# Merging two of three split passes in the mixers' feature-major gemms

## The chip, the cores and the metric

The kernel runs on one core of one Trainium2 chip. The metric is the device time of one execution in microseconds, and times are given as medians of several runs. Before the change the median of 3 runs is 1141.07 us (1139.65 to 1142.34).

## What is computed

Two transformer blocks run one after the other on 256 tokens with 1024 features, all in f32. The first mixes tokens by two kinds of attention with learned biases and has an MLP; the second has two gated FFNs around a mixer of dilated attention and an mLSTM. What the change touches are the two mixers' input projections:

```python
proj = h @ w_in[l]                       # block 1: queries, keys, values, gates
q_a, k_a, v_a, q_i, k_i, w_i, q_b, kv_b, g_b, g_br = jnp.split(proj, split_pts, axis=-1)
...
mix = (jax.nn.sigmoid(gate_a) * (o_a @ w_branch_a[l])
       + jax.nn.sigmoid(gate_b) * (o_b @ w_branch_b[l]))
x = x + mix @ w_out[l]
...
qk = jax.nn.silu(causal_depthwise_conv(qk_m, conv_w, conv_b))      # block 2
merged = jax.nn.sigmoid(g_a) * (att @ w_att_branch) + jax.nn.sigmoid(g_m) * (ml @ w_mlstm_branch)
```

Block 2's projection has the same form; it yields q, k, v of the dilated attention, the conv's input, the mLSTM's v and output gate, and two branch gates.

## The kernel before

**The split.** Every f32 product is made of three products of rounded parts: with w = hi + lo and x = xh + xl it adds hi·xh, hi·xl and lo·xh. Weights come from HBM in units of 1024 columns per partition (512 KB), issued by SyncE five units ahead (`stream_dma`). `stream_split` makes the parts two units ahead: ScalarE copies raw to `hi` (L262), VectorE subtracts to `lo` (L263). The activations lie in SBUF as `both`, of which `hi` and `lo` parts are halves that stand side by side for each k-tile.

**Three kinds of gemm.** `gemm_tok` (L305 to L307) puts tokens on the output partitions. `gemm_feat` puts features there: for each k-tile and feature tile it issues three passes of 256 columns, L349 (hi·xh), L351 (hi·xl), L352 (lo·xh), into one half of a PSUM bank; a chunk is 512 weight columns, four feature tiles, two banks. `gemm_pair`, used in the MLP and the FFNs, issues one pass of 512 columns (L368: hi against xh and xl together) and one of 256 (L369), and adds the two halves afterwards (ScalarE copy L373, VectorE add L374).

**After a gemm.** A `done` function takes the finished bank. In the mixers it multiplies by `rsB`, the norm's reciprocal root per token, on VectorE straight from PSUM: L1252 (block 2's q and k), L958 (block 1's gates), L1441 (conv input `xc`), L1470 (block 2's gates). Then follow, in block 2's q and k, the rope on GpSimd (two DMAs into `sw`, then L1260 to L1262); in the conv ScalarE's and VectorE's taps (L1446, L1449), a tanh, and GpSimd's L1453 and L1454.

**Order.** Side work (attention steps, biases, compressed keys, mLSTM heads) waits in `self.pending` and is put between k-steps by `flush`. TensorE's, VectorE's and ScalarE's instructions are then ordered by a scheduler that simulates a timeline; GpSimd and SyncE keep the program's order. Three PSUM banks (`pacc`) hold gemm results.

**Places that matter.** Block 1: the bias table goes L589 (TensorE), L591 (`tv`, VectorE), two DMAs issued by GpSimd (`tvd`, `BT`), `cmpB` (L600), `gek`, then L766; attention steps score (L835), normalize, and multiply by values (L868), the last into `oa` (L802), which is transposed (L399) and split (L406, L407) into `oaT` for the branch gemm. Block 2: L1353 multiplies the roped q and k; the mLSTM heads are multiplied into `hm` (L1521), transposed by L399.

Of the kernel before, what the change touches and what calls it, by code (L numbers as in the profile page):

```python
# [9 lines left out]
F32 = mybir.dt.float32  # L10
# [11 lines left out]
D = 1024  # L22
KT = 2
# [73 lines left out]
W_IN1 = Wt("w_in", D, [352] + [512] * 3 + [352] + [512] * 4)  # L97
# [13 lines left out]
W_G2 = Wt("ffn2_w_gate_2", D, FFW, 4)  # L111
W_U2 = Wt("ffn2_w_up_2", D, FFW, 4)
# [97 lines left out]
class Prog:  # L210
# [8 lines left out]
    def plan(self):  # L219

        o = [(W_IN1, c) for c in (4, 0, 1, 3, 2, 5, 6, 7, 8)]
# [11 lines left out]
        o += [(W_IN2, c) for c in (6, 0, 1, 2, 3, 4, 5, 7, 8, 9, 14, 15, 16, 17, 10, 18, 12, 19, 11, 13, 20, 21)]  # L233
# [124 lines left out]
    def gemm_pair(self, W, c, x, done, rate=1, delay=0):  # L358
# [16 lines left out]
        done(s)  # L375

# [176 lines left out]
    def block1_mix(self, x0, x):  # L553
        tc, nc, ap, g = self.tc, self.nc, self.ap, self.g
        with ExitStack() as es, ExitStack() as rs_:
# [78 lines left out]
            self.gemm_tok(W_IN1, 4, *xT, small_done, acc=self.psm)  # L634
# [5 lines left out]
            def d0(i, ps):  # L640
                if i == 0:
                    nc.vector.tensor_tensor(qi, ps, bc2, op=ALU.mult)
                else:
                    nc.vector.tensor_tensor(ki[64:96, :], ps[64:96, 0, :], rsB[64:96, :], op=ALU.mult)
                    nc.vector.tensor_tensor(ka[0:64, :], ps[0:64, 0, :], rsB[0:64, :], op=ALU.mult)
                    for p in (0, 32, 96):
                        nc.gpsimd.dma_start(ki[p:p + 32, :], ki[64:96, :])
                    nc.gpsimd.dma_start(ka[64:128, :], ka[0:64, :])
            self.later(rsB_job)
            self.gemm_feat(W_IN1, 0, *xT, d0)  # L650
# [130 lines left out]
            self.gemm_feat(W_IN1, 2, *xT, dq(qa))  # L781
# [173 lines left out]
            def gdone(c):  # L955
                def f(i, ps):
                    gsl = gate[:, 4 * c + 2 * i:4 * c + 2 * i + 2, :]
                    nc.vector.tensor_tensor(gsl, ps, bc2, op=ALU.mult)  # L958
                    nc.scalar.activation(gsl, gsl, AF.Tanh, scale=0.5)
                    nc.gpsimd.tensor_scalar(gsl, gsl, 0.5, 0.5, op0=ALU.mult, op1=ALU.add)  # L960
                return f
            for c in range(4):
                self.gemm_feat(W_IN1, 5 + c, *xT, gdone(c))
# [232 lines left out]
    def mixer2(self, x):  # L1196
        tc, nc, ap, g = self.tc, self.nc, self.ap, self.g
        xT, js = self.nextT
        with ExitStack() as es, ExitStack() as rs_:
# [237 lines left out]
            def cdone(c):  # L1437
                def f(i, ps):
# [143 lines left out]
```

## Time and profile before

| | |
|---|---|
| median of 3 runs | 1141.07 us |
| the profiled execution's own time | 1140.78 us |
| its span in the profile | 1139.0 us |
| mean granted TensorE clock | 0.990 |
| TensorE (PE) busy | 1112.4 us, 6848 passes |
| VectorE (DVE) busy | 766.9 us |
| ScalarE (ACT) busy | 573.3 us |
| GpSimd (POOL) busy | 143.8 us |

The span is measured on the chip between the first and last instruction; the execution's own time is 1.8 us longer. Passes of TensorE overlap, so the duration of one pass in the profile is longer than the distance from its start to the next one's. The pace is read from starts. A releaser behind "<-" is what ended an engine's wait.

### The profile page before, as it was taken

The numbers are of one execution on the slowest core, as the hardware profiler recorded it, in microseconds if no ns is written. First come the engines' busy times: TensorE is split into PE (matmuls) and PEld (weight loads), VectorE is DVE, ScalarE is ACT, GpSimd is POOL, SyncE is SP. The second block draws the span as 40 slices with busy tenths as digits, with TensorE's granted clock in tenths as the row PEclk, the third lists the DMA queues.
The fourth block names the chain that finished last, engine by engine and source line by source line (L and its number), as shares of the span: only waits on it lengthen the run. The fifth ranks groups of instructions, "written<-read, shape, count | busy, mean of one in ns | idle before, by whom it ended". The sixth has DMA issues, their size and how long they took to land.

```text
span 1139.0 us, 17655 instructions
## 1 busy us (share of the span) xinstructions
PE 1112.4 (98%) x6848; PEld 993.6 (87%) x6848; DVE 766.9 (67%) x1208; ACT 573.3 (50%) x858; POOL 143.8 (13%) x145
## 2 busy tenths in 40 slices
PE   8989999999999999999999999999999999999997
PEld 8888899888888888888878998889999987888886
DVE  6755776778764568777457676556779777776644
ACT  6324454555544446555446335555555455655542
POOL 1411230000000010000001784000323000000000
PEclk9998999999999999999999999999999998999999
DMA  8792214655555655555555655434545455555552
GB/s 294 255 195 97 65 51 146 200 187 187 191 196 173 201 181 187 186 184 192 195 167 184 192 179 167 162 119 145 185 149 166 166 188 167 185 186 186 188 179 92
DMA packets 55876, 196.91 MB, mean 173 GB/s; under 512 B 6700, under 2 KB 6972, under 8 KB 55536
## 3 DMA queue, kind: packets, MB, share of 16 engines
q1 hardware_dynamic: 52704, 186.44, 49.9%
q0 software_dynamic: 2800, 9.21, 3.3%
q8 instruction: 54, 0.88, 0.3%
q14 instruction: 30, 0.25, 0.1%
q10 hardware_dynamic: 288, 0.14, 0.1%
HBM read 192.84 MB, written 1.44 MB: 171 GB/s over the span
## 4 chain that ended last, share of the span: by engine, by line
PE 85%; POOL 5%; DMA 4%; DVE 4%; ACT 1%; issue 1%; DVEq 0%; SPq 0%; POOLq 0%; ACTq 0%
PE acc L368 20%; PE acc L369 10%; PE acc L307 9%; PE acc L306 9%; PE acc L305 9%; PE acc L349 6%; PE acc L351 6%; PE acc L352 6%; PE sm L835 2%; POOL sw L1261 2%; DMA sw<-qkT 2%; POOL qkT L1262 2%; POOL qkT L1260 1%; PE o L868 1%; DVE lo L263 1%; DMA BT<-tvd 1%
## 5 line engine op out<-in xcount | busy, mean ns | idle before, releaser
L263 DVE TENSOR_TENSOR lo<-raw,hi 128x1024 fp32r<-128x1024 f32 (+2 forms) x356 | 450.0, 1267 | 272.1 <-ACT hi L262 270.2
L262 ACT ACTIVATE hi<-raw 128x1024 fp32r<-128x1024 f32 (+2 forms) x356 | 371.5, 1045 | 432.9 <-issue 133.4
L368 PE MATMUL acc<-xs,hi 128*128 128x512 f32 x960 | 340.3, 400 | 1.3 <-DVE sum L374 1.1
L369 PE MATMUL acc<-xs,lo 128*128 128x256 f32 x960 | 269.0, 281 | 1.6 <-DVE lo L263 1.6
L368 PEld LDWEIGHTS acc<-xs,hi 128*128 128x128 f32 x960 | 180.8, 189 | 44.6 <-DVE sum L374 1.3
L349 PE MATMUL acc<-xs,hi 128*128 128x256 f32 (+1 forms) x696 | 199.8, 289 | 0.3 <-ACT hi L262 0.3
L351 PE MATMUL acc<-xs,hi 128*128 128x256 f32 (+1 forms) x696 | 199.0, 287 | 0.0
L352 PE MATMUL acc<-xs,lo 128*128 128x256 f32 (+1 forms) x696 | 198.1, 287 | 0.1
L369 PEld LDWEIGHTS acc<-xs,lo 128*128 128x128 f32 x960 | 181.9, 189 | 2.3 <-DVE lo L263 1.9
L349 PEld LDWEIGHTS acc<-xs,hi 128*128 128x128 f32 (+1 forms) x696 | 133.6, 192 | 3.7 <-issue 2.5
L351 PEld LDWEIGHTS acc<-xs,hi 128*128 128x128 f32 (+1 forms) x696 | 133.7, 192 | 2.4 <-issue 2.0
L352 PEld LDWEIGHTS acc<-xs,lo 128*128 128x128 f32 (+1 forms) x696 | 132.9, 192 | 1.6 <-issue 1.0
L306 PE MATMUL acc<-lo,hT 128*128 128x512 f32 x304 | 118.5, 390 | 0.0
L307 PE MATMUL acc<-hi,hT 128*128 128x512 f32 x304 | 118.0, 389 | 0.0
L305 PE MATMUL acc<-hi,hT 128*128 128x512 f32 x304 | 117.8, 390 | 0.0
L307 PEld LDWEIGHTS acc<-hi,hT 128*128 128x128 f32 x304 | 57.1, 188 | 11.9
L305 PEld LDWEIGHTS acc<-hi,hT 128*128 128x128 f32 x304 | 57.1, 188 | 11.8
L306 PEld LDWEIGHTS acc<-lo,hT 128*128 128x128 f32 x304 | 57.1, 188 | 11.7
L305 PE MATMUL acc<-hi,xs 128*128 128x386 f32 (+1 forms) x128 | 48.6, 381 | 1.6 <-DVE f L1129 1.5
L306 PE MATMUL acc<-lo,xs 128*128 128x386 f32 (+1 forms) x128 | 47.9, 374 | 0.0
L307 PE MATMUL acc<-hi,xs 128*128 128x386 f32 (+1 forms) x128 | 47.0, 373 | 0.0
L374 DVE TENSOR_TENSOR sum<-acc,sum 128x512 f32<-128x512 f32 x60 | 41.1, 684 | 0.0
(421 smaller groups left out, 1396.6 us busy)
## 6 DMA issues: line engine op xcount, KB each, us to landing
raw<-in_w_in SPq DMA_DIRECT2D x100, 512.0 KB, 3.5
raw<-in_ffn_w_gate SPq DMA_DIRECT2D x44, 512.0 KB, 3.4
raw<-in_ffn_w_up SPq DMA_DIRECT2D x44, 512.0 KB, 3.3
raw<-in_ffn_w_down SPq DMA_DIRECT2D x44, 512.0 KB, 3.4
raw<-in_w_mlp_in SPq DMA_DIRECT2D x32, 512.0 KB, 3.4
raw<-in_w_mlp_out SPq DMA_DIRECT2D x32, 512.0 KB, 3.3
raw<-in_w_out SPq DMA_DIRECT2D x16, 512.0 KB, 3.5
raw<-in_w_in SPq DMA_DIRECT2D x16, 386.0 KB, 3.3
```

Source lines behind the costliest of these rows:

```text
L262: nc.scalar.activation(hi[:, :n * w], raw[:, :n * w], AF.Copy)
L263: nc.vector.tensor_tensor(lo[:, :n * w], raw[:, :n * w], hi[:, :n * w], op=ALU.subtract)
L305: nc.tensor.matmul(ps[t][:, :w], xh[:, k, sl], hi, start=(k == 0), stop=False)
L306: nc.tensor.matmul(ps[t][:, :w], xh[:, k, sl], lo, start=False, stop=False)
L307: nc.tensor.matmul(ps[t][:, :w], xl[:, k, sl], hi, start=False, stop=last)
L349: nc.tensor.matmul(o, hi[:, fs], xh[:, k, :], start=(k == 0 and f % 2 == 0), stop=False, skip_group_check=True)
L351: nc.tensor.matmul(o, hi[:, fs], xl[:, k, :], start=False, stop=False, skip_group_check=True)
L352: nc.tensor.matmul(o, lo[:, fs], xh[:, k, :], start=False, stop=last, skip_group_check=True)
L368: nc.tensor.matmul(ps[:, f, :, :], hi[:, fs], x.both[:, k, :, :], start=(k == 0), stop=False)
L369: nc.tensor.matmul(ps[:, f, 0, :], lo[:, fs], x.hi[:, k, :], start=False, stop=last)
L374: nc.vector.tensor_tensor(s, ps[:, :, 0, :], s, op=ALU.add)
L835: nc.tensor.matmul(ps[:, i, :], q[pr:pr + 64, U["fts"][i], t * 128:t * 128 + 128], kk, start=True, stop=True)
```

## The change

A new function `gemm_half` does the mixers' feature-major gemms. Chunks are 256 columns wide, two feature tiles, and each tile has a PSUM bank of its own. A unit still holds 1024 columns, now four k-tiles of 256. For each k-tile there is one pass of 512 columns (hi against xh and xl) and one of 256 (lo·xh); at the tile's end ScalarE copies the half that holds hi·xl to SBUF, and VectorE adds the other half to it. When both tiles are there, `done` multiplies by `rsB` from SBUF: on VectorE as before for queries, keys and block 2's gates, on GpSimd for block 1's gates and the conv's input. 87 feature tiles change, 31 of block 1 and 56 of block 2. The branch gemms stay with `gemm_feat`, and the token-major chunks keep their widths. `flush` is called once per tile and unit, 8 times in 512 columns where `gemm_feat` called it 7 times.

```diff
-        self.kt, kts = k // 128, kt
+        self.kt = k // 128
...
+            kts = 1 << (UNIT // w).bit_length() - 1
...
-W_IN1 = Wt("w_in", D, [352] + [512] * 3 + [352] + [512] * 4)
+W_IN1 = Wt("w_in", D, [256, 96] + [256] * 6 + [352] + [256] * 8)
...
-W_IN2 = Wt("w_in_2", D, [512] * 6 + [VIF] * 4 + [512] * 12)
+W_IN2 = Wt("w_in_2", D, [256] * 12 + [VIF] * 4 + [256] * 8 + [512] * 4 + [256] * 8)
...
+    def gemm_half(self, W, c, x, dst, done, rate=1, delay=0):
+        nc = self.nc
+        w = W.widths[c]
+        nf = -(-w // 128)
+        ps = [self.pacc.tile([128, 512], F32, tag="acc", name="acc") for _ in range(nf)]
+        for u in range(len(W.off[c])):
+            kts = self.load_unit(W, c, u)
+            for f in range(nf):
+                n = min(128, w - 128 * f)
+                o = ps[f][:n, :].rearrange("p (a t) -> p a t", a=2)
+                for k, hi, lo in kts:
+                    fs = slice(f * 128, f * 128 + n)
+                    nc.tensor.matmul(o, hi[:, fs], x.both[:, k, :, :], start=(k == 0), stop=False)
+                    nc.tensor.matmul(o[:, 0, :], lo[:, fs], x.hi[:, k, :], start=False, stop=(k == W.kt - 1))
+                if kts[-1][0] == W.kt - 1:
+                    d = dst(f)
+                    nc.scalar.activation(d, o[:, 1, :], AF.Copy)
+                    nc.vector.tensor_tensor(d, o[:, 0, :], d, op=ALU.add)
+                    if f == nf - 1:
+                        done()
+                if delay <= kts[0][0]:
+                    self.flush(rate)
...
-            self.gemm_feat(W_IN1, 1, *xT, d1)
+            for c in range(2):
+                self.gemm_half(W_IN1, 2 + c, xT, lambda f: kv[:, 2 * c + f, :], lambda: kvdone(c))
...
-                    nc.vector.tensor_tensor(gsl, ps, bc2, op=ALU.mult)
+                nc.gpsimd.tensor_tensor(gsl, gsl, bc2, op=ALU.mult)
...
-            for c in range(6):
-                self.gemm_feat(W_IN2, c, *xT, qkdone(c % 2, c // 2))
+            for c in range(12):
+                i, gr, j = c // 2 % 2, c // 4, c % 2
+                self.gemm_half(W_IN2, c, xT, lambda f: qkT[i][:, gr, 2 * j + f, :], lambda: qkdone(i, gr, j))
...
-                    nc.vector.tensor_tensor(xc[:, :, 4:260], ps, rsB.unsqueeze(1).to_broadcast([128, 2, 256]),
-                                            op=ALU.mult)
+                        nc.gpsimd.tensor_tensor(th, th, bc2, op=ALU.mult)
```

The order of the instructions shifts with it. TensorE at the end of block 1, before the change: `oa` are the attention's outputs of the two token halves, `obT` the transposed parts of the other branch; the last `o<-tms,PT` stands 62 rows further up.

```order
L351 MATMUL acc<-obT_1061,hi 128x256
L352 MATMUL acc<-obT_1060,lo 128x256
L399 MATMUL sm<-ident,oa_1065 128x128
L399 MATMUL sm<-ident,oa_1066 128x128
L349 MATMUL acc<-obT_1060,hi 128x256
L351 MATMUL acc<-obT_1061,hi 128x256
L352 MATMUL acc<-obT_1060,lo 128x256
L349 MATMUL acc<-obT_1060,hi 128x256
L351 MATMUL acc<-obT_1061,hi 128x256
L352 MATMUL acc<-obT_1060,lo 128x256
L399 MATMUL tr<-ident,oa_1065 128x128
L399 MATMUL tr<-ident,oa_1066 128x128
```

And in the changed kernel, where L426 is the transpose and L900 the pass with the values:

```order
L354 MATMUL acc<-obT_972,lo 128x256
L351 MATMUL acc<-obT_972,hi 128x256
L900 MATMUL o<-tms,PT 128x64 x8
L353 MATMUL acc<-obT_973,hi 128x256
L354 MATMUL acc<-obT_972,lo 128x256
L351 MATMUL acc<-obT_972,hi 128x256
L353 MATMUL acc<-obT_973,hi 128x256
L354 MATMUL acc<-obT_972,lo 128x256
L426 MATMUL sm<-ident,oa_977 128x128
L426 MATMUL sm<-ident,oa_978 128x128
L426 MATMUL tr<-ident,oa_977 128x128
L426 MATMUL tr<-ident,oa_978 128x128
```

The last pass with the values now stands 5 branch passes ahead of the transposes, which come in a row; before, more than 60 branch and gate passes lay between, and the transposes were spread among branch passes.

TensorE in block 2, before: the first product of roped q and k (`qkT`, L1353) stands among the value gemm's passes, behind the whole gemm of q and k.

```order
L305 MATMUL acc<-hi,xs 128x386
L306 MATMUL acc<-lo,xs 128x386
L307 MATMUL acc<-hi,xs 128x386
L1353 MATMUL sm<-qkT_5816,qkT_5815 128x256
L305 MATMUL acc<-hi,xs 128x386
L306 MATMUL acc<-lo,xs 128x386
```

In the changed kernel (L1383 is that product, L393 and L394 the gemm of q and k) it stands inside the gemm of q and k, after 120 of its 192 pairs; the second stands after 184.

```order
L394 MATMUL acc<-xs,lo 128x256
L393 MATMUL acc<-xs,hi 128x512
L394 MATMUL acc<-xs,lo 128x256
L1383 MATMUL sm<-qkT_5640,qkT_5639 128x256
L393 MATMUL acc<-xs,hi 128x512
L394 MATMUL acc<-xs,lo 128x256
```

So TensorE now comes to the first two of these products earlier, and to the third with 103 instead of 96 passes of the value gemm behind it.

GpSimd in the conv, two tiles' worth of instructions, before (`xc` is the conv's padded input, `y` its sum, `qkm` its result):

```order
L1440 MEMSET xc 128x2x4
L1453 TENSOR_SCALAR xc<-xc 128x2x256
L1454 TENSOR_TENSOR qkm_7595<-xc,y 128x512
L1440 MEMSET xc 128x2x4
L1453 TENSOR_SCALAR xc<-xc 128x2x256
L1454 TENSOR_TENSOR qkm_7595<-xc,y 128x512
```

And in the changed kernel, where the multiply by `rsB` (L1475) stands ahead of each pair:

```order
L1471 MEMSET xc 128x2x4
L1475 TENSOR_TENSOR xc<-xc,rsB 128x2x256
L1486 TENSOR_SCALAR xc<-xc 128x2x256
L1487 TENSOR_TENSOR qkm_7287<-xc,y 128x512
L1471 MEMSET xc 128x2x4
L1475 TENSOR_TENSOR xc<-xc,rsB 128x2x256
L1486 TENSOR_SCALAR xc<-xc 128x2x256
L1487 TENSOR_TENSOR qkm_7287<-xc,y 128x512
```

GpSimd issues the multiply between the clearing of the padding and the last two steps of the same pair of tiles; the next pair's multiply stands behind these.

## Rows read from the trace of the kernel before

**Rows 1.** The page, part 1: busy us, share of the span, instructions of each engine.
```profile
PE 1112.4 (98%) x6848; PEld 993.6 (87%) x6848; DVE 766.9 (67%) x1208; ACT 573.3 (50%) x858; POOL 143.8 (13%) x145
```

**Rows 2.** Waits of TensorE: line, releaser, us in total, times, longest.
```profile
PE sm L766 <- DVE gek L757: 6.1, 1, 6.1
PE sm L305 <- ACT hi L262: 2.3, 1, 2.3
```

**Rows 3.** One line (L349, 625 to 680 us), then the timeline of TensorE there: start, us.
```profile
L349 PE MATMUL acc<-xs,hi x153: 283/283/283, 625.0 to 679.7; 128*128 128x256 f32 x153
...
639.74 0.28 PE L349 MATMUL acc<-xs,hi 128*128 128x256 f32 x1
639.86 0.28 PE L351 MATMUL acc<-xs,hi 128*128 128x256 f32 x1
```

**Rows 4.** The same for L368: two stretches, and the timeline of TensorE at 1000 us.
```profile
L368 PE MATMUL acc<-xs,hi x146: 392/394/395, 249.6 to 299.9; 128*128 128x512 f32 x146
...
L368 PE MATMUL acc<-xs,hi x199: 395/398/403, 969.7 to 1039.7; 128*128 128x512 f32 x199
...
999.73 0.40 PE L368 MATMUL acc<-xs,hi 128*128 128x512 f32 x1
999.96 0.28 PE L369 MATMUL acc<-xs,lo 128*128 128x256 f32 x1
1000.08 0.40 PE L368 MATMUL acc<-xs,hi 128*128 128x512 f32 x1
```

**Rows 5.** Windows: us, busy us of PE, PEld, DVE, ACT, POOL, clock, DMA share.
```profile
776.00:881.00 105.00, 104.92 (x849) 103.71 (x849) 82.42 (x139) 57.46 (x85) 29.10 (x33) 1.00 0.50 162
825.00:881.00 56.00, 55.92 (x441) 54.80 (x440) 47.82 (x89) 31.59 (x50) 17.19 (x19) 1.00 0.47 153
```

**Rows 6.** Lines by form; first L406 and L407 alone, then whole run, then lo in two stretches.
```profile
L406 ACT ACTIVATE attT<-tr x2: 378/391/404, 783.6 to 784.1; 128x256 fp32r<-128x256 f32 x2
...
L407 DVE TENSOR_TENSOR obT<-tr,obT x4: 372/414/415, 164.6 to 170.5; 128x256 fp32r<-128x256 f32 x4
...
L1184 DVE TENSOR_TENSOR sum<-sum,rsB 128x512 f32<-128x512 f32 x22 | 15.2, 691 | 0.6
...
L1441 DVE TENSOR_TENSOR xc<-acc,rsB 128x512 f32<-128x512 f32 x8 | 5.5, 688 | 0.3
...
L1454 POOL TENSOR_TENSOR qkm<-xc,y 128x512 f32<-128x512 f32 x8 | 14.6, 1822 | 0.7
...
L263 DVE TENSOR_TENSOR lo<-raw,hi 128x1024 fp32r<-128x1024 f32 x32 | 40.7, 1272 | 16.2 <-ACT hi L262 16.2
...
L263 DVE TENSOR_TENSOR lo<-raw,hi 128x1024 fp32r<-128x1024 f32 x36 | 44.0, 1225 | 24.1 <-ACT hi L262 23.9
```

**Rows 7.** Q/K stage: a window, timelines of POOL and PE, lo by form (620 to 690), L305.
```profile
680.00:700.00 20.00, 18.00 (x103) 17.58 (x102) 15.13 (x11) 10.34 (x14) 17.26 (x9) 1.00 0.48 153
...
696.93 2.96 POOL L1262 TENSOR_TENSOR qkT<-qkT,sw 32x1024 f32<-32x1024 f32 x1
...
699.94 0.95 PE L1353 MATMUL sm<-qkT,qkT 128*128 128x256 f32 x2 [2.00 <-POOL qkT L1262]
...
L263 DVE TENSOR_TENSOR lo<-raw,hi 128x1024 fp32r<-128x1024 f32 x20 | 32.5, 1634 | 15.3 <-ACT hi L262 15.3
...
L305 PE MATMUL acc<-hi,xs x32: 333/339/525, 680.1 to 697.3; 128*128 128x386 f32 x32
```

**Rows 8.** Timelines of DVE, POOL and PE around the stop before L766.
```profile
60.30 0.53 DVE L591 TENSOR_TENSOR tv<-sm,rest 16x384 f32<-16x384 f32 x1
...
86.69 0.38 POOL L600 COPY cmpB<-BT 128x120 f32<-128x120 f32 x1 [14.65 <-DMA BT<-tvd]
...
87.63 0.40 PE L766 MATMUL sm<-gek,csk 128*64 128x16 f32 x4 [6.11 <-DVE gek L757]
```

**Rows 9.** Timeline of TensorE at the end of block 1's attention.
```profile
174.15 1.89 PE L868 MATMUL o<-tms,PT 128*128 128x64 f32 x16
...
183.25 0.38 PE L399 MATMUL sm<-ident,oa 128*128 128x128 f32 x2
```

More of the change, by code (lines that the diff above doesn't have):

```diff
@@ L219, in plan @@
     def plan(self):
-        o = [(W_IN1, c) for c in (4, 0, 1, 3, 2, 5, 6, 7, 8)]
+        o = [(W_IN1, c) for c in (8, 0, 1, 2, 3, 6, 7, 4, 5, *range(9, 17))]
         for c in range(2):
@@ L638, in block1_mix, with qidone, kkdone @@
             wi = lambda t, h: tms[:, t, 320 + h:321 + h]
[L640 to L648, printed above, removed]
+            def qidone():
+                nc.vector.tensor_tensor(qi, qi, bc2, op=ALU.mult)
+            kk_ = bp.tile([128, 256], F32, name="kk")
+            def kkdone():
+                nc.vector.tensor_tensor(ki[64:96, :], kk_[64:96, :], rsB[64:96, :], op=ALU.mult)
+                nc.vector.tensor_tensor(ka[0:64, :], kk_[0:64, :], rsB[0:64, :], op=ALU.mult)
+                for p in (0, 32, 96):
+                    nc.gpsimd.dma_start(ki[p:p + 32, :], ki[64:96, :])
+                nc.gpsimd.dma_start(ka[64:128, :], ka[0:64, :])
             self.later(rsB_job)
-            self.gemm_feat(W_IN1, 0, *xT, d0)
+            self.gemm_half(W_IN1, 0, xT, lambda f: qi[:, f, :], qidone)
+            self.gemm_half(W_IN1, 1, xT, lambda f: kk_[0:96, :], kkdone)
             M = cp.tile([128, 2, 256], F32, name="M")
@@ L780, in block1_mix @@
                        lambda: cmp2(0), lambda: cmp2(1))
-            self.gemm_feat(W_IN1, 2, *xT, dq(qa))
+            queries(qa, 4)
             self.flush()
@@ L953, in block1_mix, with gdone @@
             gate = cp.tile([128, 16, 256], F32, name="gate")
-            def gdone(c):
-                def f(i, ps):
-                    gsl = gate[:, 4 * c + 2 * i:4 * c + 2 * i + 2, :]
-                    nc.vector.tensor_tensor(gsl, ps, bc2, op=ALU.mult)
[L959 to L963, printed above, removed]
+            def gdone(gsl):
+                nc.gpsimd.tensor_tensor(gsl, gsl, bc2, op=ALU.mult)
+                nc.scalar.activation(gsl, gsl, AF.Tanh, scale=0.5)
+                nc.gpsimd.tensor_scalar(gsl, gsl, 0.5, 0.5, op0=ALU.mult, op1=ALU.add)
+            for c in range(8):
+                gsl = gate[:, 2 * c:2 * c + 2, :]
+                self.gemm_half(W_IN1, 9 + c, xT, lambda f: gsl[:, f, :], lambda: gdone(gsl))
             self.flush()
@@ new lines, in conv, with done @@
+                    th = xc[:, :, 4:260]
+                    def done():
+                        nc.gpsimd.tensor_tensor(th, th, bc2, op=ALU.mult)
+                        y = cvp.tile([128, 2, 256], F32, tag="y", name="y")
+                        for f in range(2):
+                            ff = 4 * c + 2 * i + f
+                            nc.scalar.activation(y[:, f, :], xc[:, f, 4:260], AF.Identity, bias=cb[:, ff:ff + 1],
+                                                 scale=cw[:, ff, 3:4])
+                            for j in range(3):
+                                nc.vector.scalar_tensor_tensor(y[:, f, :], xc[:, f, 1 + j:257 + j],
+                                                               cw[:, ff, j:j + 1], y[:, f, :], op0=ALU.mult,
+                                                               op1=ALU.add)
+                        nc.scalar.activation(th, y, AF.Tanh, scale=0.5)
+                        nc.gpsimd.tensor_scalar(th, th, 0.5, 0.5, op0=ALU.mult, op1=ALU.add)
+                        nc.gpsimd.tensor_tensor(qkm[c][:, 2 * i:2 * i + 2, :], th, y, op=ALU.mult)
@@ L1456, in mixer2 @@
+                    self.gemm_half(W_IN2, 16 + 2 * c + i, xT, lambda f: th[:, f, :], done)
             g2p = rpool("gates2", 1)
@@ L1477, in mixer2 @@
             hs = self.small(8, "hs")
-            self.gemm_feat(W_IN2, 10, *xT, cdone(0))
-            self.gemm_feat(W_IN2, 18, *xT, gfeat(gta, 0))
-            self.gemm_feat(W_IN2, 12, *xT, cdone(2))
-            self.gemm_feat(W_IN2, 19, *xT, gfeat(gta, 1))
+            conv(0)
+            gfeat(gta, 28, 0)
+            conv(2)
+            gfeat(gta, 28, 1)
             ws = {}
```

108 lines of the change are left out of this document (49 added, 59 removed).

## The prediction

> **What bounds the kernel now.** I read the busy totals first: TensorE is busy 1112.4 of 1139.0 us, VectorE 67%, ScalarE 50%, GpSimd 13% [rows 1]. So only the pace of TensorE's passes and the few places where it stands still can move the time. Next the table of TensorE's waits [rows 2]: one stop of 6.1 us (L766, on the copy into gek), the next 2.3 us, and no other line is over that; there is little to gain here. Third the pace of the passes in the timeline. In `gemm_feat` (L349, L351, L352) starts stand 0.12 us apart: 639.74, 639.86 and so on [rows 3]. In `gemm_pair` a 512-column pass starts at 999.73, its 256-column partner at 999.96, the next 512 at 1000.08 [rows 4]. Last the busy time by stage [rows 5], to see how much room VectorE and GpSimd have where the change loads them. Above 98% busy, a pass that goes away is time that goes away, unless something else then ends last.
>
> **The passes.** 87 feature tiles of 8 k-tiles are 696 triples. Before: three passes of 256 columns; now one of 512 and one of 256, so the same 768 columns, and one pass fewer. Price of a triple: 153 L349 from 625.0 to 679.7 are 152 steps in 54.7 us, 359.9 ns [rows 3]. Price of the new pair, from the same form in `gemm_pair`: 146 L368 from 249.6 to 299.9 are 145 steps in 50.3 us, 346.9 ns; 199 from 969.7 to 1039.7 are 198 steps in 70.0 us, 353.5 ns [rows 4]. I take the middle, 350.2, since the two stretches are equally like the new code: 9.7 ns x 696 = **6.7 us saved**; the ends are 6.4 and 13.0 ns, 4.5 to 9.0 us.
> [...]
>
> **The new evacuation.** Each tile now ends in a ScalarE copy of one half and a VectorE add of the other. The nearest rows are the 128x256 PSUM copy, 0.37 to 0.39 us (L406), and the 128x256 PSUM add, 0.42 (L407) [rows 6]: 87 x 0.38 = 33 us on ScalarE (573 busy before), 87 x 0.42 = 37 us on VectorE. The multiply by rsB stays, but reads SBUF: 0.691 against 0.688 us for the same shape (L1184, L1441) [rows 6], nothing. Sixteen of them (8 gate, 8 conv) move to GpSimd, which takes 11 us off VectorE and puts 16 x up to 1.8 us (L1454) on GpSimd [rows 6]. I cost all this at nothing by itself: the copy and add need under 1 us, some 2 behind one lo of 1.27 [rows 6], and by the written order a bank is wanted again two half-tiles (8 pairs, 2.8 us) after its last pass. If that cover is gone, each tile costs up to the difference. The price appears where TensorE waits for something that VectorE or GpSimd finishes late; there are four such places.
>
> **Q/K stage.** Here six ropes follow one another on GpSimd, which is busy 17.26 of 20 us at the end; the last addition runs 696.93 to 699.89, and TensorE then starts L1353 at 699.94 after 2.0 us of waiting [rows 7]. So the stage ends with the ropes, and the 192 triples' 1.9 us are no gain. By the order, 103 instead of 96 value passes now stand before the pass that needs the last rope (32 L305 are 31 steps of three passes in 17.2 us, 0.185 us a pass [rows 7]: 7 of them are 1.3 us more done under the wait). Against that the first rope starts later: it follows the fourth tile's multiply, which now stands behind a copy and an add (0.8 us; its pass is 0.3 earlier), and lo, rope and the SBUF multiply disturb one another (lo takes 1.63 us here, 1.23 elsewhere [rows 6, 7]); I take 1.0 us. So this stage gives 0.3 instead of 1.9: **+1.6** in the sum, from +0.6 (ropes not late) to +3.1 (2.5 late). The first two of these passes now stand inside the Q/K gemm; where they wait for the second and fourth rope, that wait only takes the place of the later one.
>
> **The stop of 6.1 us.** Its chain is TensorE's L589, VectorE's tv at 60.30, two DMAs one after the other that GpSimd issues (tvd, BT), cmpB at 86.69 after 14.65 us of waiting for the second, then gek and L766 at 87.63 [rows 8]. After tv nothing in it shrinks. L589's counterpart now stands after 88 triples instead of 94, and 42 follow it before the stop instead of 40. If tv comes as much earlier as TensorE does (6 triples and 88 cheaper ones, 3 us), the stage keeps its gain; if VectorE, which is busy right up to tv with its adds on top, is as late as before, its 2.3 us (31 tiles of the first block) are lost. With both in play I take **+0.5**, from -0.5 to +2.3.
>
> **Tail of block 1.** Before, the last probability-value passes (L868, 174.15) are 9.1 us ahead of the oa transposes (L399, 183.25), and gate and branch passes fill the time [rows 9]. In the new order 5 branch passes (0.6 us) stand between, then eight transposes in a row, then two passes on oaT. What is needed between is the multiply into oa (0.69 us, a PSUM multiply as L1441, which may stand behind a lo), and behind the transposes a copy and a subtract (0.38 + 0.42): 0.7 + 0.8 - 0.6 = 0.9 without a queue, 2.2 with a lo in front. I take **+1.3**, 0.5 to 3.
>
> **Conv and the second branch.** VectorE is busy 82.42 of 105 us from 776 to 881, and 47.82 of 56 in its second part [rows 5]. In that part 441 passes are 147 triples, 18 tiles: 18 x 0.42 - 4 x 0.69 = +4.8, so 52.6 us in about 54.6. It still fits, barely; what it finishes last, hm for its transposes, has 92 passes (11.0 us) of cover in the new order instead of 107 (12.8). I take **+0.7**, 0 to 3.
>
> **Sum.** -6.7 + 1.6 + 0.5 + 1.3 + 0.7 = -2.6 us on the profiled execution of 1140.78, which lies 0.29 under the median of 1141.07. The median should move by the same: **1138.5 us**. 0.2% of 1141.07 is 2.3 us, about what a measurement can tell from no change.
>
> **Rivals.** *The saving arrives whole.* VectorE has a third of its time free on average, and three of the four late places may be absorbed by waits that exist already. With 347 ns pairs -9.0, with 350 -6.7, less the rope's 1.6: -5.1 to -7.4, about 1135. Speaks for it: TensorE idles only 1139.0 - 1112.4 = 27 us in all before [rows 1]. Against: the ropes leave no gap.
> *The passes save little.* If a pass's fixed part is small in these stages, the pairs come out at 357 ns, half way from the slower stretch to three passes: 3 ns x 696 = 2.1 saved; the 2.5 of the other terms stay and the rope's shrinks to 0.4: +0.8, about 1141.9, no change. [...]
> *GpSimd's multiplies hold VectorE up* (slower). In the conv stage VectorE would be at 52.6 of 54.6 us; four conv multiplies of 1.82 us each lie in it on GpSimd. If VectorE stands still for them, 52.6 + 7.3 = 59.9, 5.3 over, and the hm chain behind it loses another 1 to 2: -2.6 + 6.7 = +4.1, 1145.2. It decides once what they hold up exceeds 2.0 us, about a quarter of their time. For it: under the ropes lo takes a third longer [rows 6, 7]. Against: in the conv stage, with GpSimd at 29.1 us already, lo's mean is 1.27 us, 0.05 above the undisturbed one [rows 5, 6].
> [...]
> *The change doesn't do what it says:* the new order has the merged passes in all 696 places, so no chance is given to it.
>
> **Chances.** The forecast (-1 to -4.5) 0.42, half of it beyond 2.3 us; saving whole 0.27; little saved 0.08; held up 0.23. Faster 0.21 + 0.27 = 0.48; same 0.21 + 0.08 = 0.29; slower 0.23. The range takes in the whole saving at 347 ns with half of the rope's loss (-8.1, 1133.0) and the third rival with some more (1146.5). The forecast's own range is 1136.5 to 1140.
>
> **What would show it.** Right: pairs (L393 to L393) 347 to 354 ns apart; L1383's last wait for POOL about where it was, near 697 to 701 us of the span; a new wait of 1 to 2 us at the oa transposes near 180 us; the stop at L798 still 5 to 8 us; VectorE over 92% busy in the conv stage without TensorE waiting on it. Wrong: pairs at 358 or more; TensorE waits on `acc` for the new add or on lo in the conv or gate stage, with lo well over 1.3 us; or no wait at the tail and the stop shrunk, with the time at 1135 or under.

## The result: slower, outside the range

| | before | after |
|---|---|---|
| median (4 runs each) | 1140.49 us (1139.65 to 1142.34) | 1151.9 us (1149.44 to 1152.56) |
| ratio to before, 95% interval | | 1.0074 [1.0053, 1.0096] |
| profiled execution, its span | 1140.78, 1139.0 | 1151.83, 1150.0 |

Predicted were 1138.5 us and a range of 1133.0 to 1146.5. The page of after, part 1, answers to [rows 1]:

```profile
PE 1109.9 (97%) x6152; PEld 953.4 (83%) x6152; DVE 802.7 (70%) x1278; ACT 597.9 (52%) x944; POOL 165.2 (14%) x161
```

The 696 passes are gone (6848 to 6152), but TensorE stands idle 1150.0 - 1109.9 = 40.1 us where it was 26.6. The table of its waits (us in total, times, longest), beside [rows 2]:

```profile
PE sm L798 <- DVE gek L789: 10.7, 1, 10.7
PE acc L393 <- DVE qkT L398: 5.8, 8, 1.2
PE acc L393 <- DVE gtm L398: 2.9, 1, 2.9
PE tr L426 <- DVE xs L430: 2.2, 2, 1.8
...
PE sm L1383 <- POOL qkT L1292: 0.6, 1, 0.6
```

The stop was 6.1 us and is 10.7. Two lines of more than 1 us are new: passes that wait for the add of the new evacuation (L398), in the Q/K gemm and in the gates. The wait for the last rope (L1353, now L1383) fell from 2.0 to 0.6 us. No line names the oa transposes. Where each stage's first pass starts, by the two traces, gives this account:

| stretch | before | after | difference |
|---|---|---|---|
| block 1, to its output gemm | 206.4 | 206.9 | +0.5 |
| of it: to the stop / the stop / behind it | 81.3 / 6.4 / 118.8 | 78.7 / 10.9 / 117.3 | -2.6 / +4.6 / -1.5 |
| output gemm, MLP, first FFN (code unchanged) | 404.2 | 405.8 | +1.6 |
| Q/K gemm | 69.4 | 76.3 | +6.8 |
| value gemms behind it | 96.4 | 93.7 | -2.6 |
| conv, gates | 104.6 | 105.9 | +1.3 |
| both branch gemms | 36.7 | 40.2 | +3.5 |
| the rest | 221.2 | 221.3 | 0 |

The pace of the new pairs is the predicted one [rows 4]. In the Q/K gemm's timeline of after (start, us, engine, line), four steps from L393 to L393 take 1.41 us, 353 ns each; in other stretches, as from 629 to 642 us, they take 347:

```profile
660.83 0.40 PE L393 MATMUL acc<-xs,hi 128*128 128x512 f32 x1
661.06 0.28 PE L394 MATMUL acc<-xs,lo 128*128 128x256 f32 x1
661.18 0.40 PE L393 MATMUL acc<-xs,hi 128*128 128x512 f32 x1
...
662.24 0.40 PE L393 MATMUL acc<-xs,hi 128*128 128x512 f32 x1
```

Busy time by stage, after: Q/K, values, conv with gates, attention branch (us, then PE, PEld, DVE, ACT, POOL, clock, DMA share, GB/s):

```profile
612.70:688.90 76.20, 70.43 (x392) 59.34 (x392) 69.44 (x79) 33.90 (x50) 40.50 (x22) 1.00 0.55 177
688.90:782.60 93.70, 92.20 (x496) 80.05 (x495) 60.39 (x93) 49.22 (x73) 18.41 (x11) 1.00 0.47 154
782.60:888.60 106.00, 102.97 (x582) 89.26 (x581) 89.02 (x159) 64.46 (x114) 38.89 (x36) 0.98 0.48 156
888.60:904.00 15.40, 14.71 (x114) 14.17 (x113) 11.01 (x28) 9.09 (x20) 7.17 (x8) 1.00 0.58 192
```

In the Q/K gemm VectorE is busy 69.4 of 76.2 us; in before it was 49.0 of 69.4:

```profile
610.60:680.00 69.40, 69.40 (x580) 69.32 (x579) 49.02 (x54) 26.70 (x27) 41.64 (x22) 1.00 0.62 197
```

What fills it stands in its lines by form for after's window (busy us, mean ns | idle before):

```profile
L265 DVE TENSOR_TENSOR lo<-raw,hi 128x1024 fp32r<-128x1024 f32 x23 | 43.6, 1908 | 6.1 <-ACT hi L264 5.9
L1282 DVE SCALAR_TENSOR_TENSOR qkT<-qkT,rsB 128x512 f32<-128x512 f32 x11 | 14.8, 1342 | 0.4
L398 DVE TENSOR_TENSOR qkT<-acc,qkT 128x256 f32<-128x256 f32 x23 | 9.5, 414 | 0.0
```

The adds cost what was foreseen, 0.41 us. The multiply from SBUF takes 1.34 where 0.69 was expected [rows 6], lo 1.91. Their distribution (min/median/max ns) tells more than the mean; lo in after, 612.7 to 688.9:

```profile
L265 DVE TENSOR_TENSOR lo<-raw,hi x26: 946/1224/3422, 611.7 to 688.8; 128x1024 fp32r<-128x1024 f32 x23, 128x772 fp32r<-128x772 f32 x3
```

and in before, 620 to 690, which is the stretch of [rows 7]:

```profile
L263 DVE TENSOR_TENSOR lo<-raw,hi x27: 950/1226/3321, 619.4 to 689.8; 128x1024 fp32r<-128x1024 f32 x20, 128x772 fp32r<-128x772 f32 x7
```

Of those with 1024 columns, 15 of 23 in after take 1.21 to 1.23 us and the other eight 2.92 to 3.42; in before 11 of 20 take 1.21 to 1.23 and the other nine are spread from 1.30 to 3.32. The timeline of after shows what the long ones stand beside, first VectorE's:

```profile
647.21 0.69 DVE L1282 SCALAR_TENSOR_TENSOR qkT<-qkT,rsB 128x512 f32<-128x512 f32 x1
647.81 0.42 DVE L398 TENSOR_TENSOR qkT<-acc,qkT 128x256 f32<-128x256 f32 x1
649.08 6.26 DVE L265 TENSOR_TENSOR lo<-raw,hi 128x1024 fp32r<-128x1024 f32 x2 [0.85 <-ACT hi L264]
655.27 0.41 DVE L398 TENSOR_TENSOR qkT<-acc,qkT 128x256 f32<-128x256 f32 x1
655.71 2.43 DVE L1282 SCALAR_TENSOR_TENSOR qkT<-qkT,rsB 128x512 f32<-128x512 f32 x1
```

GpSimd's in the same stretch:

```profile
648.52 2.40 POOL L1290 TENSOR_TENSOR qkT<-qkT,cs 32x1024 f32<-32x1024 f32 x1 [2.97 <-DMA sw<-qkT]
650.89 3.37 POOL L1291 TENSOR_TENSOR sw<-sw,cs 32x1024 f32<-32x1024 f32 x1
654.34 3.25 POOL L1292 TENSOR_TENSOR qkT<-qkT,sw 32x1024 f32<-32x1024 f32 x1
```

And TensorE's next pass that needs the add's bank:

```profile
655.73 0.51 PE L393 MATMUL acc<-xs,hi 128*128 128x512 f32 x1 [0.61 <-DVE qkT L398]
```

Two lo that need 2.4 us take 6.26 beside the rope; the multiply beside the rope's last step takes 2.43 instead of 0.69; the add, one of whose inputs is in PSUM, keeps its 0.41 beside the same step, but stands in line behind lo. Taken one by one, the first lo takes 2.92 us and ends at 652.00, 1.1 us after the rope's first step, the second takes 3.42 and ends at 655.34, 1.1 us after its second step. An undisturbed lo takes 1.21 to 1.23 in all, so by an estimate from these rows most of each ran only after a step of the rope had ended.

### The profile page after: what moved, and what is told of

It is laid out like the page before. It is cut to its first block, busy times and chain, and to the rows that moved or that the text cites. A ratio compares the mean times of both kernels' runs of the same rounds, so it can differ in the third digit from the quotient of the medians.

```text
span 1150.0 us, 16402 instructions
## 1 busy us (share of the span) xinstructions
PE 1109.9 (97%) x6152; PEld 953.4 (83%) x6152; DVE 802.7 (70%) x1278; ACT 597.9 (52%) x944; POOL 165.2 (14%) x161
## 4 chain that ended last, share of the span: by engine, by line
PE 85%; DVE 4%; DMA 3%; POOL 3%; ACT 2%; issue 2%; DVEq 0%; POOLq 0%; ACTq 0%
PE acc L370 20%; PE acc L393 11%; PE acc L371 10%; PE acc L309 9%; PE acc L307 9%; PE acc L308 9%; PE acc L394 5%; DVE lo L265 3%; DMA BT<-tvd 2%; PE sm L867 2%; PE acc L351 2%; PE acc L354 2%; PE acc L353 1%; ACT hi L264 1%; PE o L900 1%
## 5 line engine op out<-in xcount | busy, mean ns | idle before, releaser
L265 DVE TENSOR_TENSOR lo<-raw,hi 128x1024 fp32r<-128x1024 f32 (+3 forms) x355 | 459.5, 1299 | 249.4 <-ACT hi L264 247.9
L264 ACT ACTIVATE hi<-raw 128x1024 fp32r<-128x1024 f32 (+3 forms) x355 | 370.7, 1046 | 389.4 <-issue 133.1
L393 PE MATMUL acc<-xs,hi 128*128 128x512 f32 (+1 forms) x696 | 253.3, 405 | 9.0 <-DVE qkT L398 5.8
L394 PE MATMUL acc<-xs,lo 128*128 128x256 f32 (+1 forms) x696 | 197.2, 286 | 0.0
L393 PEld LDWEIGHTS acc<-xs,hi 128*128 128x128 f32 (+1 forms) x696 | 131.2, 190 | 43.5 <-DVE qkT L398 8.5
L394 PEld LDWEIGHTS acc<-xs,lo 128*128 128x128 f32 (+1 forms) x696 | 132.4, 190 | 3.8 <-issue 2.3
L1072 POOL TENSOR_TENSOR xg<-x,row 128x512 f32<-128x512 f32 x4 | 6.1, 1514 | 201.9 <-DVE x L1070 201.9
L375 ACT ACTIVATE sum<-acc 128x512 f32<-128x512 f32 x60 | 34.8, 581 | 0.0
```

The source lines that it names most:

```text
L264: nc.scalar.activation(hi[:, :n * w], raw[:, :n * w], AF.Copy)
L265: nc.vector.tensor_tensor(lo[:, :n * w], raw[:, :n * w], hi[:, :n * w], op=ALU.subtract)
L375: nc.scalar.activation(s, ps[:, :, 1, :], AF.Copy)
L393: nc.tensor.matmul(o, hi[:, fs], x.both[:, k, :, :], start=(k == 0), stop=False)
L394: nc.tensor.matmul(o[:, 0, :], lo[:, fs], x.hi[:, k, :], start=False, stop=(k == W.kt - 1))
```

## Experiments

The first run undoes the change in the Q/K gemm alone, the second in the conv and gates, the third in block 1; each takes its functions, widths and order of units from before. Ratios are to the kernel before, run beside it on the same chip, where its median lay between 1141.7 and 1143.7 us; a run without a ratio is a single execution.

```diff
-            for c in range(12):
-                i, gr, j = c // 2 % 2, c // 4, c % 2
-                self.gemm_half(W_IN2, c, xT, lambda f: qkT[i][:, gr, 2 * j + f, :], lambda: qkdone(i, gr, j))
+            for c in range(6):
+                self.gemm_feat(W_IN2, c, *xT, qkdone(c % 2, c // 2))
```

> The changed kernel, with the Q/K stage alone put back to gemm_feat (512-column chunks, three passes, multiply from PSUM). Theory A (GpSimd's rope additions and multiplies hold up VectorE's instructions that read two SBUF operands, lo and the new multiply, so the new adds stand in line and banks come free late): the waits of TensorE on qkT adds (5.8 us) go, the Q/K gemm takes 69.4 us again instead of 76.2, Q/K and value stage together give back 4.2 us: about 1147.5. Theory B (VectorE has simply too much to do, with or without GpSimd): the same. Rival: the loss moves on into the value stage, where the ropes end: 1150 or more.

1148.36 us, 1.0048 [1.0029, 1.0067]. Q/K 69.35 us again, Q/K with the values 164.1 (before 165.8, after 170.0), no wait for qkT's adds. The Q/K gemm's part of the loss is 4 to 6 us by these stretches, 3 by the ratio; what causes it, this run doesn't tell.

```diff
-            conv(0)
+            self.gemm_feat(W_IN2, 16, *xT, cdone(0))
...
-            gfeat(gta, 28, 0)
+            self.gemm_feat(W_IN2, 24, *xT, gfeat(gta, 0))
```

> The changed kernel, with the conv and block 2's gates alone put back to gemm_feat (their multiply from PSUM on VectorE). If their evacuation and the multiply moved to GpSimd cost what the trace shows between 782 and 929 us (1.3 in the conv stage, 2.7 in the attention branch, 0.8 in the mLSTM branch), 4.8 us come back: about 1147. If the passes' saving there outweighs it, the time goes up by 1 to 3.

1144.99, 1.0027 [1.0009, 1.0045]. From the conv's start to the mLSTM branch's end it takes 141.3 us, as before; after took 146.1. So conv and gates cost 4.8.

```diff
-W_IN1 = Wt("w_in", D, [256, 96] + [256] * 6 + [352] + [256] * 8)
+W_IN1 = Wt("w_in", D, [352] + [512] * 3 + [352] + [512] * 4)
```

> The changed kernel, with block 1 alone put back to gemm_feat. By the trace block 1 as a whole ends 0.5 us later than before, with the stop before gek 4.6 us longer and the rest some 4 shorter. If the longer stop comes from the new order, it is back at 6 us and block 1 ends as before: 0.5 us less, 1151.4. If the longer stop is chance (the bias table's DMAs took 24.2 us instead of 19.4), the changed kernel's other runs show it at 6 to 11 us without a reason in the code, and this one is slower than the changed kernel by the passes' 2 to 4 us.

1150.91, 1.0079 [1.0049, 1.0108]. The stop is 5.7 us again, yet block 1 ends at 206.05, 0.9 earlier only: the longer stop had eaten what the passes gave.

**Is it GpSimd?** The rope's arithmetic is left out, its DMAs stay.

```diff
-                nc.gpsimd.tensor_tensor(q[0:32], q[0:32], bc4(0), op=ALU.mult)
-                nc.gpsimd.tensor_tensor(sw, sw, bc4(1), op=ALU.mult)
...
-                nc.gpsimd.tensor_tensor(q[0:32], q[0:32], sw, op=ALU.add)
```

> The changed kernel without GpSimd's three arithmetic instructions of each rope: q and k stay without rotation, the DMAs into sw remain. Theory A: lo in the Q/K stage takes 1.23 us again (1.91 in the changed kernel), the multiply by rsB 0.69 (1.34), TensorE's waits on the qkT adds go below 1 us in all and the Q/K gemm takes about 67 to 68 us instead of 76.2. Theory B (VectorE is overloaded by the adds themselves): lo at 1.23 too, but waits on the adds of 3 us or more stay.

1142.3 us. Q/K takes 70.0 us, and VectorE's lines from 612.7 to 688.9 read:

```profile
L265 DVE TENSOR_TENSOR lo<-raw,hi 128x1024 fp32r<-128x1024 f32 x23 | 28.2, 1225 | 16.4 <-ACT hi L264 16.3
...
L1282 DVE SCALAR_TENSOR_TENSOR qkT<-qkT,rsB 128x512 f32<-128x512 f32 x12 | 8.3, 692 | 0.4
```

The same instructions cost 1225 and 692 ns once GpSimd is busy for 4.8 of 70.0 us (40.5 of 76.2 in after), and TensorE's waits for these adds fall from 5.8 to 1.4 us. That GpSimd holds VectorE up in this stage, and TensorE with it, is shown. The stage did not come down to the 67.5 us that its 192 cheaper triples would give.

```diff
-                nc.gpsimd.tensor_tensor(gsl, gsl, bc2, op=ALU.mult)
+                nc.vector.tensor_tensor(gsl, gsl, bc2, op=ALU.mult)
...
-                        nc.gpsimd.tensor_tensor(th, th, bc2, op=ALU.mult)
+                        nc.vector.tensor_tensor(th, th, bc2, op=ALU.mult)
```

> The changed kernel, with the 16 multiplies by rsB that went to GpSimd (block 1's gates, the conv's input) back on VectorE, still from SBUF. Theory A (GpSimd's instructions hold VectorE's two-operand ones, and the adds behind them): in the conv stage TensorE's wait on the gtm add (2.9 us) goes and the stage from the conv to the end of the mLSTM branch, 146.1 us in the changed kernel and 141.3 before, comes down by 2 us or more. Rival: VectorE has no room there (89.0 of 106 us busy), 8 more multiplies of 0.69 us make it worse, and the stage grows by 1 to 3.

1147.75, 1.0036 [1.002, 1.0052]. Conv to mLSTM takes 141.2 us, 4.9 less, although VectorE now does eight multiplies more; the 2.9 us wait of the gates falls to 0.2, and another of 1.15 us appears before a pass of the conv. TensorE's waits between the conv and the output gemm sum to 4.0 us in after, 1.6 here and none in before. What had happened in the 2.9 us is in the timeline of after, VectorE's rows:

```profile
860.94 1.28 DVE L468 TENSOR_SCALAR h_h<-h0v 128x4 f32<-128x4 f32 x1
862.10 0.15 DVE L467 TENSOR_SCALAR h0r<-h_t 128x4 int32<-128x4 int32 x1
...
862.28 1.15 DVE L470 TENSOR_TENSOR h_t<-h0r 128x4 f32<-128x4 f32 x1
863.36 0.41 DVE L398 TENSOR_TENSOR gtm<-acc,gtm 128x256 f32<-128x256 f32 x1
```

beside GpSimd's, and then TensorE's:

```profile
860.89 1.27 POOL L1487 TENSOR_TENSOR qkm<-xc,y 128x512 f32<-128x512 f32 x1
862.16 1.26 POOL L1475 TENSOR_TENSOR xc<-xc,rsB 128x512 f32<-128x512 f32 x1
863.83 0.50 PE L393 MATMUL acc<-xs,hi 128*128 128x512 f32 x1 [2.92 <-DVE gtm L398]
```

Two tiny instructions of the mLSTM, 0.15 to 0.17 us elsewhere, take 1.28 and 1.15 us beside one GpSimd multiply each, and end when it ends (at 862.22 beside 862.16, at 863.43 beside 863.42); the add and TensorE wait behind them. The lo of this stage are longer too: 12 of the 32 with 1024 columns take 1.30 to 2.31 us in after, four in before.

Behind the wait stands a second price. TensorE's granted clock is 1.00 through the wait and 0.50 from 864.49 to 867.90 us:

```profile
864.49:867.90 3.41, 3.41 (x12) 2.89 (x11) 3.34 (x11) 1.85 (x3) 0.00 (x0) 0.50 0.00 0
```

Pairs start 0.64 us apart there instead of 0.35:

```profile
865.39 0.63 PE L393 MATMUL acc<-xs,hi 128*128 128x512 f32 x1
865.81 0.41 PE L394 MATMUL acc<-xs,lo 128*128 128x256 f32 x1
866.03 0.63 PE L393 MATMUL acc<-xs,hi 128*128 128x512 f32 x1
```

That is 1.5 us lost, an estimate from these starts. Neither before nor this run has such a stretch between the conv and the output gemm. Before has one elsewhere, behind its 2.0 us wait for the last rope, which after lacks:

```profile
700.25:703.66 3.41, 3.41 (x10) 2.95 (x9) 3.37 (x8) 1.37 (x3) 0.00 (x0) 0.50 0.60 197
```

In block 1 the same edit missed: it ends at 210.70, where after ends at 206.94 and four other runs with the same block 1 code end at 207.6 to 207.8. So 3 to 4 us went there, and GpSimd was the better place; 0.5 us of it is a wait at the oa transposes, the rest no wait names.

**Multiply from PSUM instead.** The add goes back into the bank and the multiply reads it there, first in Q/K, then (with Q/K undone) in conv and gates.

```diff
-                    nc.vector.tensor_tensor(d, o[:, 0, :], d, op=ALU.add)
+                    if mul:
+                        nc.vector.tensor_tensor(o[:, 0, :], o[:, 0, :], d, op=ALU.add)
+                        nc.vector.scalar_tensor_tensor(d, o[:, 0, :], mul[0], mul[1], op0=ALU.mult, op1=ALU.mult)
...
-                nc.vector.scalar_tensor_tensor(qs, qs, 128.0 ** -0.5 if i == 0 else 1.0, bc2, op0=ALU.mult,
-                                               op1=ALU.mult)
```

> The changed kernel, with the add of the Q/K tiles written back into PSUM and the multiply by rsB taken from there, tile by tile, so that neither reads two operands from SBUF. Theory A: the multiply is no longer stretched (1.34 us for 512 columns in the changed kernel; now about 0.42 for 256), while lo still is (1.9 us); TensorE's waits on the adds fall from 5.8 to 3 to 5 us. If GpSimd held VectorE whatever the operands are, the multiply would be stretched as before.

1150.51. The multiply isn't stretched any more, as VectorE's line for the Q/K window says:

```profile
L400 DVE SCALAR_TENSOR_TENSOR qkT<-acc,rsB 128x256 f32<-128x256 f32 x22 | 9.3, 425 | 0.8
```

Yet Q/K takes 77.4 us: a bank is now held until rsB is there, and at the start TensorE waits for what rsB is made from (`tr L579 <- rt L578`, 3.2 us).

> The changed kernel with Q/K put back to gemm_feat and, in the conv and block 2's gates, the add written back to PSUM and the multiply taken from there on VectorE (no multiply on GpSimd, none with two SBUF operands). Theory A: from the conv to the end of the mLSTM branch the stage takes 139 to 141.5 us (146.1 in the changed kernel, 141.3 before); the whole lies within 3 us of before, its rest being block 1's stop. If VectorE's share of work alone is the limit there, it stays at 144 or more.

1146.91, 1.0034 [1.002, 1.0049]. Conv to mLSTM 144.5 us, a miss: TensorE waits 2.8 us for xc's multiply, which now holds the bank, and 1.5 for a result of the conv from GpSimd.

**The stop.** Three runs asked whether its place, its buffers or its start matter: kk taken out of its own buffer; only block 1 changed, with that edit; and, on top, the table's side job put earlier in the program.

```diff
-            kk_ = bp.tile([128, 256], F32, name="kk")
+            kk_ = qb[:, 0, :]
```

> The changed kernel with the new 128x256 tile kk not allocated in its pool: its values go through the first quarter of qb, which is written later. Every instruction stands in the same order. While only the bias table moves, its packets take about 500 ns in the kernels with the new block 1 and about 400 in those with the old one, for the same bytes. If that comes from where tiles lie in SBUF, the stop before gek falls from 10 to 11 us to some 6 and the time by 4 to 5. If it comes from the order of work or of the transfers, the stop stays at 10 to 11.5.

1150.57, 1.0065 [1.0044, 1.0086], stop 10.8: where kk lies is not the reason.

> Only block 1 in the new form (with kk in qb as in x6), block 2 as before. Block 1 as a whole ended 0.5 us later than before in the changed kernel with a stop 4.6 us longer. If the stop is mended, 3 to 5 us faster than before; if not, within 1.5 us of it.

1142.49, 0.9984 [0.9963, 1.0006], stop 10.1: no faster than before by itself.

```diff
+            self.pending.appendleft(bias_job)
             for c in range(2):
                 self.gemm_half(W_IN1, 2 + c, xT, lambda f: kv[:, 2 * c + f, :], lambda: kvdone(c))
...
-            self.later(bias_job)
+            self.later(cmpb_job)
```

> Block 1 alone in the new form (as x7), and the bias table's job put at the head of the queue before the key and value gemm (its two copies into cmpB stay where they were). If the stop before gek is nothing but the table's DMAs started too late, it goes from 10.1 us to under 3, and 5 to 8 us come off x7: 6 to 10 us faster than before. If the table's 2 MB then hold up the weight units of the key and value gemm, half of that or less.

1140.58, 0.998 [0.9953, 1.0006]. The stop is gone and block 1 ends at 200.59, but the time, expected 6 to 10 us below before, is not clearly below that of the kernel without the early start. The profile is of its fastest execution, 1134.24 us, so 200.59 flatters it.

> The kernel before with the bias table's job put forward in the same way. If the stop is only a matter of when the table starts, it goes here too, from 6.1 us to under 2: 3 to 5 us faster than before. The difference between this one and x9 is then what the merged passes of block 1 are worth without the stop: 31 tiles x 8 x 10 to 12 ns = 2.5 to 3 us.

The same edit on the kernel before: 1140.07, 0.9972 [0.9957, 0.9987], block 1 ends at 205.40. A wait of 3.9 us for GpSimd's blkk takes the stop's place.

```diff
-        self.stream_dma(self.n_use + DMA_AHEAD)
+        n = self.n_use
+        self.stream_dma(min(n + 7, 22) if 9 <= n <= 19 else n + DMA_AHEAD)
```

> The changed kernel, with one more raw buffer and the weight units that block 1 issues around the bias table fetched up to two units earlier, so that hardly any unit is on its way together with the table. Theory: weight units and the table share the 16 DMA engines, 3.6 MB in 24 us; without the units the table's 2.1 MB at the 131 GB/s it has when alone take 16 us, and the stop falls from 10.7 to 3 to 5 us. Rival: the table alone sets it (its packets at 500 ns whoever else is there): then it lands at most 2 us earlier.

1154.21, stop 10.6; weights were still issued in the table's time, at 62.17, 67.80 and 74.02 us, so this settled nothing.

The chain itself, VectorE's and GpSimd's timelines of after (beside [rows 8]), then the transfers' issue in before:

```profile
57.80 0.53 DVE L618 TENSOR_TENSOR tv<-sm,rest 16x384 f32<-16x384 f32 x1
58.62 0.60 POOL L621 DMA_DIRECT2D tvd<-tv  x1 [7.21 <-DVE tv L618]
64.44 4.55 POOL L623 DMA_DIRECT2D BT<-tvd  x8 [5.21 <-DMA tvd<-tv]
88.68 0.38 POOL L627 COPY cmpB<-BT 128x120 f32<-128x120 f32 x1 [19.38 <-DMA BT<-tvd]
...
67.25 4.47 POOL L596 DMA_DIRECT2D BT<-tvd  x8 [5.53 <-DMA tvd<-tv]
```

tv came 2.5 us earlier (57.80), but the eight transfers into BT took 88.68 - 64.44 = 24.2 us, where before they took 86.69 - 67.25 = 19.4. While the table is alone on the queues, all DMA engines are busy and move 133 GB/s in after:

```profile
70.00:76.00 6.00, 6.00 (x40) 5.39 (x40) 3.73 (x16) 2.10 (x4) 0.00 (x0) 1.00 1.06 133
```

and 175 in before:

```profile
72.00:78.00 6.00, 6.00 (x53) 6.00 (x52) 2.71 (x8) 1.18 (x2) 0.04 (x1) 1.00 1.03 175
```

Each of the eight writes 16 neighbouring partitions. The next runs write the same bytes to every eighth partition instead, for which the addresses that each transfer reads in `tvd` change too (a step of 16 * 384 - 8 for 16 * 384 - 1): in the changed kernel, in the one with block 1 alone changed, and in the one before.

```diff
-                    nc.gpsimd.dma_start(BT[16 * i:16 * i + 16, :, :],
-                                        bass.AP(tensor=tvd.tensor, offset=tvd.offset + 127 - 16 * i,
-                                                ap=[[16 * 384 - 1, 16], [384, 16], [1, 256]]))
+                    nc.gpsimd.dma_start(BT[i:128:8, :, :],
+                                        bass.AP(tensor=tvd.tensor, offset=tvd.offset + 127 - i,
+                                                ap=[[16 * 384 - 8, 16], [384, 16], [1, 256]]))
```

> The changed kernel, with each of the eight transfers that read the bias table writing every eighth partition instead of 16 neighbouring ones; the same bytes, the same number of transfers. Theory: the 16 engines, in step on one transfer, all write to 16 neighbouring partitions and get in each other's way (500 ns a packet), unless weight packets in between have put them out of step (400 ns, the old order). Then packets take 400 ns or less, the stop falls from 10.7 to 6 us or less, and 4 to 8 us come off. Rival: the slower packets come from the source side or the mix of transfers: no change, within 1.5 us.

1142.32, 1.0009 [0.999, 1.0028]: one DMA's addresses give back nearly all of the loss. Its waits and GpSimd's timeline:

```profile
PE sm L798 <- DVE gek L789: 2.0, 1, 2.0
```

```profile
64.06 4.52 POOL L623 DMA_DIRECT2D BT<-tvd  x8 [5.22 <-DMA tvd<-tv]
79.63 0.37 POOL L627 COPY cmpB<-BT 128x120 f32<-128x120 f32 x1 [10.74 <-DMA BT<-tvd]
```

15.6 us instead of 24.2, at 216 GB/s:

```profile
70.00:74.00 4.00, 4.00 (x27) 3.61 (x27) 2.44 (x12) 1.44 (x3) 0.00 (x0) 1.00 1.04 216
```

> Block 1 alone in the new form (x7) with the transfers spread as in x14. By the theory 4 to 8 us off x7, 5 to 8 us faster than before; by the rival as x7, within 3 us of before.

1134.52, 0.993 [0.9902, 0.9957]; block 1 ends at 199.45. It is faster than before, and its ratio is the lowest of the study.

> The kernel before with the transfers spread as in x14. By the theory the stop falls from 6.1 us to 0 to 4: 2 to 5 us faster than before. By the rival no change.

1138.19, 0.9959 [0.9941, 0.9978]; block 1 ends at 203.65. So with the transfers mended the merged passes of block 1 seem worth 4.2 us by the two traces, 3.7 by the two medians on one chip. But the intervals of the two ratios overlap, and the trace of this run alone has 3.4 us at a granted clock of 0.50 from 38.8 us on, where passes of 256 columns start 0.21 us apart instead of 0.12: 1.5 us of the 4.2 by an estimate from these starts.

> The changed kernel itself. If the stop (10.7 us) and the MLP's pace (352.7 ns) belong to the kernel they come out within 1 us and 0.5 ns of that; if the pace is chance of an execution it may be 346.2.

The changed kernel once more: 1153.17, stop 10.4, the MLP's pairs 352.6 ns apart as in the first profile. Both came again in a second execution.

**The three mends together.** The spread transfers, the conv's multiply on VectorE and Q/K undone, all in one:

> The changed kernel with Q/K back on gemm_feat (x1), the conv's multiply on VectorE (half of x5) and the table's transfers spread over the partitions (x14). If the three mechanisms are the whole loss: block 1 ends 7 to 8.5 us earlier than before (x14, x15), Q/K and the value stage take what they took before or up to 1.5 us less, conv to mLSTM branch 141.2 (x5): 6 to 9 us faster than before, about as x15. If something of the change still costs, it is slower than x15 by 2 us or more.

1135.82, 0.9951 [0.9937, 0.9965]: block 1 ends at 199.87, Q/K with values takes 167.7 us, conv to mLSTM 141.1. The time goes from 1.0074 to a gain, but less than the 6 to 9 us expected (1141.71 to 1135.82), and the account does not close: conv to mLSTM takes what it took before although its 256 pairs should save 2.5 us, and Q/K with values takes 1.9 more than before in the old code. Nor is the gain that of the merged passes: the kernel before has 0.9959 from the spread transfers alone, and the intervals overlap.

## Why the prediction was wrong, step by step

- **The passes** (-6.7): right. The pairs run at 347 to 353 ns, so the saving was there and was lost elsewhere.
- **The new evacuation** failed: "I cost all this at nothing by itself ... some 2 behind one lo of 1.27". The add's own 0.41 us was right; what it can stand behind was not. The mean of 1.63 us for lo under the ropes was read as "takes a third longer", when that mean was made of eleven at 1.2 and nine from 1.3 to 3.3, of which the longest took 2.1 us more than the eleven. The argument against the third rival read an average. Pricing the multiply at "nothing" failed for the same reason: its 0.691 us from SBUF (L1184) came from the FFNs, where GpSimd did nothing beside it. Under the ropes five of twelve took 2.42 to 2.64 us, the others 0.69.
- **Q/K** (+1.6): Q/K and values together came out at +4.2, which already holds these passes' own saving of about 1.9; the term is about +6. The ropes' end, on which I put it, cost less than before (0.6 us of waiting for 2.0, and no stretch at a granted clock of 0.50 behind it); the adds behind lo, at nothing in the sum, cost 5.8.
- **The stop** (+0.5, to +2.3): +4.6 in the stage, -2.6 ahead of it. "After tv nothing in it shrinks" left out that something could grow. tv was earlier by 2.5 us, near the 3 of the hopeful case; the transfers gave 4.8 back. That the stop hangs on how long they take is shown by the runs that spread them. Those change the partitions and the source addresses at once, so which of the two counts is not shown, and why the same transfers ran at 175 GB/s in the old order and 133 in the new is open. That the DMA engines get in each other's way there was the author's guess, which no run shows.
- **The tail of block 1** (+1.3): no wait; the term is 0.
- **Conv and branches** (+0.7, to 3): measured +4.8 with the passes' saving (256 triples, 2.5 us) already in it, so a term of about +7: 4.0 us of waits, some 1.5 of the lower clock behind the longest, the rest not located. Here the third rival was right in mechanism: GpSimd's multiplies hold VectorE up, and moving them back gives 4.9, of it 2.3 in waits and the 1.5 of the clock. In the longest wait two tiny mLSTM instructions took 1.28 and 1.15 us where they take 0.16 elsewhere; what the longer lo cost is not shown.
- **The MLP** (not in the sum): +1.6 in unchanged code. Its pairs run at 346 to 347 ns in twelve of the nineteen profiles of this study and at 353 in seven, both of the changed kernel among these; the cause is open.

With the passes' own 2.4 us taken out, block 1 as a whole lost 2.9. Then -6.7 for the passes, 2.9, 6 for Q/K, 7 for the conv and branches and 1.6 for the MLP make 10.8 of the 11.0 us by which the span grew.

The mechanism with the chance of 0.23 thus happened, in two places, and a second loss that no rival held, the longer transfers, came on top.

## What to carry to other kernels

Read the minimum, median and maximum of an instruction beside a GpSimd one, not its mean, and count what queues behind the long ones. Moving an operand of VectorE's from PSUM to SBUF, or work to GpSimd, is priced by that, not by the instruction's time alone: here the multiply from SBUF, 0.69 us elsewhere, took 1.34 in the mean beside the ropes. To a wait of TensorE add what it then runs at the lower clock, here 3.4 us at 0.50 behind waits of 2.0 and 2.9 us. Before blaming a wait on an order, compare the length and rate of each DMA in its chain: here one line of addressing was worth as much as the whole change was meant to be.

## What the runs showed of the hardware

- Eight transfers of the same bytes, each into 16 partitions: 133 GB/s in after and 175 in before, where the 16 are neighbours, 216 in the changed kernel where they are every eighth. The source addresses differ with the partitions, so which of the two makes the difference is not shown.
- Beside a GpSimd multiply of 1.26 us a VectorE instruction on 128x4 elements took 1.15 us (0.16 elsewhere); beside the rope's steps of 2.4 to 3.4 us a lo on 128x1024 took up to 3.42 (1.21 to 1.23 in 15 of 23).
- Behind TensorE's 2.92 us wait in the conv and gates the granted clock was 0.50 for 3.4 us, and pairs started 0.64 us apart instead of 0.35.
